# A hybrid convolution and retention step on one core: first weights in other pieces, taps scaled one sum later, the last head's norm ahead of its gate, and the feed-forwards' first job by k tiles

## The chip, the core and the metric

The kernel runs on one core of one Trainium2 chip. The core has a matrix engine (TensorE, PE in the profile; PEld is its weight load), VectorE (DVE), ScalarE (ACT), GpSimd (POOL) and SyncE (SP), which work side by side and meet through semaphores; each takes its own instructions in order. Matrix products end in PSUM, everything else lies in SBUF, and inputs come from memory by DMA, which SP, ScalarE or GpSimd start. The metric is the device time of one execution, in microseconds (us), lower is better.

## The reference

One inference step of a two-layer decoder over 544 tokens (512 of a prompt, 8 sequences of 4 sample tokens) with 1024 features, all in fp32:

```
x = x + short_conv_mixer(rmsnorm(x))      # layer 0: b, c, h = split(x @ w_in); u = c*h
                                          # y = sum_j w_conv[j] * u shifted by j; out = (b*y) @ w_out
x = x + swiglu(rmsnorm(x))                # (silu(x @ w_gate) * (x @ w_up)) @ w_down
x = x + retention_mixer(rmsnorm(x))       # layer 1: 4 heads, chunks of 128 tokens, a state S per head,
                                          # a norm over each head's output, a silu gate, @ w_out
x = x + swiglu(rmsnorm(x))
y = rmsnorm(x)
```

Returned are y for both groups of tokens, the last convolution inputs and the retention states.

## The kernel before

**Numbers.** An fp32 value is held as two reduced fp32 parts, a rounded high part (wh, oh, h: a copy by ScalarE, L202 or L326) and the low rest (wl, ol, l: a subtraction by VectorE, L203 or L327). A product of two values is three matmuls: high by high, high by low, low by high. Activations are stored feature by token; a matmul takes a 128x128 weight tile and half of the tokens, 272 (HT). `split` makes both parts; `mixed` makes the high part on ScalarE, then the low part half on VectorE and half through a DMA of GpSimd that adds the source to the negated high part (L328, L329).

**Jobs of seven products.** Most projections pair two 128-row blocks of weights and two blocks of operands and compute the 2x2 block product with seven products in place of eight (class `Job`, L375; products named 1 to 7, summed in L397). `weights7` (L331) makes the sums of weight blocks on VectorE (L347 to L350) and their parts. A job runs as `begin` (product 1), `middle` (5, 6, 2 in an order given to `run`, L433, for the first job, then 7) and `end` (3, 4); `take` names the results u1, u2, p5, c11, u3, c12 and c21, which ScalarE copies (L456) or VectorE adds to others (L458). Each product runs over four pairs of k tiles (KP = 4; KT = 8 k tiles of 128 features).

**Order.** The kernel is a straight program without loops on the chip. A scheduler orders each engine's queue from the order of the text, the tile pools' buffers and explicit constraints (`tc.issue_after(x.ins)`: behind instruction x). A constraint in one place can therefore also move instructions some distance away.

**Start and convolution (L464 to L681).** `start` (L481) loads x by eight k tiles (L502) and the first three weight blocks in pieces: k tile 0, tiles 1 to 3, tiles 4 to 7. All but one of the weight pieces go through SP's queue (L157), which lets eight loads be under way: a further one waits for the load eight places ahead. `split_x` scales and splits each k tile of x (L221, L222). The three projections then go k tile by k tile (L187). Two more `products` (L522) run on whole pieces, each piece split in one go (1024 wide). `square_sum` (L229) adds squares of x (L234 to L240) for the norm, `rms_scale` (L259) sums them over the features by matmuls (L275), takes the power on GpSimd (L250) and spreads it by matmuls (L256). The rest of the stage are jobs: for each pair of feature blocks one for c, one for h, and one for b. After an h job, VectorE forms u = c*h (L635, L636) and `taps` (L568) the convolution's sum y (L572, L574), which it then multiplies by the norm factor R (L583, L584); the b job's result is multiplied by y at its end (L589, L590).

**Feed-forwards (L684 on, one for each layer).** `operand` (L775) makes the parts for a k tile: scaling of x (L782), sums and differences of its blocks (L317 to L320), and their parts, 816 and 544 wide (L202, L203). A k tile of x is itself finished only by the stage ahead (L305 adds its projection). A loop (L884 to L890) calls `operand` and `square_sum` for each k tile in the order PAIRED[layer], whose last two are 6 and 7; the last square sum stands behind the last operand's parts. The first job's middle products run in the order 5, 2, 6 in the second layer and 5, 6, 2 in the first, each over all four k pairs.

**Retention (heads loop, L1603 to L1704).** For each head, chunks of 128 tokens are projected, multiplied, normalised (`normal`, L1419; its multiplication is L1422), gated (`gated`, L1447; L1460) and transposed; `states_update` (L1524) adds to the states (L1541). The function `inside` (L1684) is called from the next projection and holds the gating of chunk 2, the normal of chunk 3 and its state update, in this order. Normals use tiles of the tag yn, two buffers.

Of the kernel before, what the change touches and what calls it, by code (L numbers as in the profile page):

```python
# [12 lines left out]
P = 128  # L13
D = 1024
KT = D // P
SEQ = 512
# [36 lines left out]
def hybrid_decode_kernel(ctx: ExitStack, tc: tile.TileContext, a: dict, o: dict):  # L53
# [276 lines left out]

    def weights7(src1, src2, sw, n, adding=False, spare=None, first=1, fourth=False, whole=False):  # L331

# [13 lines left out]
        s2, s1 = w2[:, :n], w2[:, n:]  # L346
        nc.vector.tensor_add(s1, a21, a22)  # L347
        nc.vector.tensor_sub(s2, s1, a11)
        nc.vector.tensor_sub(a21, a11, a21)
        nc.vector.tensor_sub(w4, a12, s2)  # L350

# [7 lines left out]
        p3 = parts2(2 * n)  # L359
        mixed(*p3, w3, src2)  # L360
        p4 = parts2(n, sw, ("h4", "l4"))
# [13 lines left out]
    class Job:  # L375
# [14 lines left out]

        def product(self, out, which, first):
            wh, wl = self.w[which]
            for j, k in enumerate(self.ks):
                c = slice(j * P, (j + 1) * P)
                bh, bl = self.operand(k, which)
                for i, (w, b) in enumerate(((wh, bh), (wh, bl), (wl, bh))):
                    last = nc.tensor.matmul(  # L397
                        out, w[:, c], b,
                        start=(first and j == 0 and i == 0), stop=(j == len(self.ks) - 1 and i == 2),
                        skip_group_check=True,  # L400
                    )
                if which not in (5, 6, 2):
                    with tc.issue_after(last.ins):
                        next(self.weave, None)

        def begin(self):
            self.a = bank()[:, :HT]
            self.product(self.a, 1, True)
            self.take("u1", self.a)

        def middle(self):
            for which in self.order:
                if which == 6:
                    self.product(self.a, 6, False)
                    self.take("u2", self.a)
                elif which == 5:
                    self.c = self.third()[:, :HT]
                    self.product(self.c, 5, True)
                    self.take("p5", self.c)
                else:  # L420
                    self.b = bank()[:, :HT]
                    self.product(self.b, 2, True)
                    self.take("c11", self.b)
# [9 lines left out]
    def run(jobs, order, after, steps):  # L433
# [4 lines left out]
        for i, job in enumerate(jobs):  # L438
# [7 lines left out]
            after(i)  # L446

    def summed(dst, finish):


        def take(what, src):
# [5 lines left out]
            elif what in more:  # L457
                nc.vector.tensor_add(more[what], more[what], src)  # L458
            finish(what, src)
# [5 lines left out]
    with ExitStack() as c0:  # L465
# [15 lines left out]
        def start():  # L481


            pieces = [load_piece(a["cvin"][j], KT * P, parts=True) for j in range(3)]
            parts = [slice(0, P), slice(P, KP * P), slice(KP * P, KT * P)]
            nc.sync.dma_start(x[0], a["xT"][0])
# [13 lines left out]
            for kt in range(1, KT):  # L500
                steps.append(lambda kt=kt: split_x(kt, g_mix(0, kt)))
                nc.sync.dma_start(x[kt], a["xT"][kt])  # L502
                if kt in (1, 3):
                    for p in pieces:
                        p[2](parts[1 + kt // 3])
                        steps.append(lambda p=p, kt=kt: p[3](parts[1 + kt // 3]))
            last = steps[0]()
# [14 lines left out]
        def products(f, js, weave=iter(())):  # L522
            pts = []
            for j in js:
                wh, wl = load_piece(a["cvin"][3 * f + j], KT * P)
                pt = psum()
# [40 lines left out]

        def taps(f, scaled=True):  # L568

# [10 lines left out]
            )  # L580
            if scaled:
                r = R.rearrange("p a b -> p (a b)").unsqueeze(1).to_broadcast([P, 2, T])
                nc.vector.tensor_mul(y[:, :, NSLOT:], y[:, :, NSLOT:], r[:, :, :SEQ])  # L583
                nc.vector.tensor_mul(slots(y)[..., :DS], slots(y)[..., :DS], tokens(r))  # L584
            return y

        def mixed_in(b, y, f):
# [37 lines left out]
        def job(f, j):  # L625
            def take(what, src):
                if what != "c21":
                    return
# [29 lines left out]
        with ExitStack() as order:  # L658
            for last in (last_x[0], last_x[1], last_square[0]):
                order.enter_context(tc.issue_after(last.ins))  # L660
            for k in range(KP):
                operand_sums(k)
        mixed_in(b, taps(0, False), 0)
        run(jobs, (2, 5, 6), lambda i: None, iter(()))
# [19 lines left out]
    def ffn(layer, next_gain, then=None):  # L684
        with ExitStack() as c1:
# [198 lines left out]
            for kt in PAIRED[layer]:  # L884
                made = operand(kt)
                with ExitStack() as held:
                    if kt == KT - 1:
                        held.enter_context(tc.issue_after(made.ins))
                        held.enter_context(tc.issue_after(last_low[0].ins))
                    square_sum(kt, None, add=nc.vector)  # L890
            def after(i):
# [3 lines left out]
            steps = rms_scale(rest=9)  # L895
            run(jobs, (5, 2, 6) if layer else (5, 6, 2), after, steps)
            drain(steps)
# [223 lines left out]
    with ExitStack() as c2:  # L1121
# [296 lines left out]

        def normal(src, mv, rs):  # L1419

            yn = tp.tile([P, DV], F32, tag="yn", name=nm("yn"), bufs=2)
            last_normal[0] = nc.vector.tensor_scalar(yn, src, mv[:, 0:1], rs, op0=ALU.subtract, op1=ALU.mult)  # L1422
# [180 lines left out]
        for h in range(NH):  # L1603
# [79 lines left out]

            def inside():  # L1684
                with tc.issue_after(last_product[0].ins):
                    gated(h, st, yn2, 2)
                st["yn3"] = normal(p3, last, scale)
                states_update(h, st, 3, last_normal[0])
# [133 lines left out]
```

## Time and profile before

| what | value |
|---|---|
| median of 3 runs | 1389.73 us (1389.16 to 1390.19) |
| the profiled execution | 1392.42 us, span 1390.6 us |
| granted TensorE clock | 0.999 |
| busy: TensorE, VectorE, ScalarE, GpSimd | 1378.3, 1132.9, 823.4, 218.6 us |
| memory read and written | 191.31 and 28.42 MB |

The page counts an engine as busy while an instruction of its own is in it; TensorE's matmuls overlap, and a 128x128 by 272 matmul that waits for nothing starts every 0.125 us though its own time is about 0.29. A row of the timeline begins with its start and its duration in us, counted from the start of the span; then engine, line, operation, and output <- inputs with partitions x elements. In brackets stands how long the engine idled before it and what released it. "x3" is a run of three such instructions, and the duration is that of the run. A stall of TensorE of a microsecond is 0.07% of the time.

### The profile page before, as it was taken

The numbers are of one execution on the slowest core, as the hardware profiler recorded it, in microseconds if no ns is written. First come the engines' busy times: TensorE is split into PE (matmuls) and PEld (weight loads), VectorE is DVE, ScalarE is ACT, GpSimd is POOL, SyncE is SP. The second block draws the span as 40 slices with busy tenths as digits, with TensorE's granted clock in tenths as the row PEclk, the third lists the DMA queues.
The fourth block names the chain that finished last, engine by engine and source line by source line (L and its number), as shares of the span: only waits on it lengthen the run. The fifth ranks groups of instructions, "written<-read, shape, count | busy, mean of one in ns | idle before, by whom it ended". The sixth has DMA issues, their size and how long they took to land.

```text
span 1390.6 us, 26494 instructions
## 1 busy us (share of the span) xinstructions
PE 1378.3 (99%) x10427; PEld 1314.9 (95%) x10427; DVE 1132.9 (81%) x1925; ACT 823.4 (59%) x1284; POOL 218.6 (16%) x249
## 2 busy tenths in 40 slices
PE   9999999999999999999999999999999999999998
PEld 8999999999999999999978887887899999999997
DVE  6988789898989878777868586586799898989875
ACT  6666567767667656767641413224377767667654
POOL 0111012212221213211200000000112212221212
PEclk9999999999999999999999999999999999999999
DMA  6476346777777754777566455475766777777752
GB/s 208 113 179 154 121 108 154 171 174 171 152 183 166 165 126 122 195 180 221 175 237 230 148 187 202 134 258 183 220 137 153 171 172 174 154 180 167 164 111 88
DMA packets 99005, 233.15 MB, mean 168 GB/s; under 512 B 9760, under 2 KB 33456, under 8 KB 98496
## 3 DMA queue, kind: packets, MB, share of 16 engines
q1 hardware_dynamic: 68032, 167.47, 38.5%
q0 software_dynamic: 28400, 56.09, 23.5%
q10 hardware_dynamic: 2448, 7.91, 1.5%
q8 instruction: 81, 1.33, 0.4%
q14 instruction: 44, 0.36, 0.1%
HBM read 191.31 MB, written 28.42 MB: 158 GB/s over the span
## 4 chain that ended last, share of the span: by engine, by line
PE 94%; DVE 3%; DMA 1%; ACT 1%; issue 0%; POOL 0%; SPq 0%; DVEq 0%; ACTq 0%; POOLq 0%
PE sm L397 43%; PE mm L397 16%; PE mm L187 14%; PE sm L187 5%; PE sm L1267 2%; PE sm L1268 2%; PE sm L1269 2%; PE sm L175 2%; PE sm L176 1%; PE sm L177 1%; PE sm L1517 1%; PE mm L1278 1%; PE mm L1535 1%; PE mm L1445 1%; DMA w<-in_cvin_dram 0%
## 5 line engine op out<-in xcount | busy, mean ns | idle before, releaser
L397 PE MATMUL sm<-oh,wh 128*128 128x272 f32 x856 | 247.8, 290 | 2.0 <-ACT oh L202 1.5
L397 PE MATMUL sm<-ol,wh 128*128 128x272 f32 x856 | 246.2, 288 | 0.0
L397 PE MATMUL sm<-oh,wl 128*128 128x272 f32 x856 | 246.0, 287 | 0.0
L202 ACT ACTIVATE h<-w 128x1024 fp32r<-128x1024 f32 (+3 forms) x170 | 136.5, 803 | 91.1 <-PE mm L397 77.6
L203 DVE TENSOR_TENSOR l<-w,h 128x1024 fp32r<-128x1024 f32 (+3 forms) x170 | 153.6, 905 | 21.8 <-ACT h L202 19.7
L397 PEld LDWEIGHTS sm<-oh,wh 128*128 128x128 f32 x856 | 161.3, 188 | 3.5 <-ACT oh L202 1.8
L397 PEld LDWEIGHTS sm<-oh,wl 128*128 128x128 f32 x856 | 161.1, 188 | 0.0
L397 PEld LDWEIGHTS sm<-ol,wh 128*128 128x128 f32 x856 | 160.8, 188 | 0.2
L326 ACT ACTIVATE wh<-w 128x1024 fp32r<-128x1024 f32 (+1 forms) x132 | 131.8, 998 | 48.8 <-PE sm L397 40.8
L202 ACT ACTIVATE wh<-w 128x1024 fp32r<-128x1024 f32 (+3 forms) x78 | 70.0, 903 | 126.8 <-PE mm L187 61.2
L397 PE MATMUL sm<-parts,wh 128*128 128x272 f32 x736 | 142.6, 288 | 0.0
L329 POOL DMA_DIRECT2D wl<-in_ffgu_dram x87 | 81.9, 941 | 323.2 <-ACT wl L328 141.4
L397 PEld LDWEIGHTS sm<-parts,wh 128*128 128x128 f32 x736 | 115.5, 188 | 0.0
L397 PE MATMUL mm<-oh,h 128*128 128x272 f32 x396 | 114.0, 288 | 0.0
L397 PE MATMUL mm<-oh,l 128*128 128x272 f32 x396 | 113.4, 286 | 0.0
L397 PE MATMUL mm<-ol,h 128*128 128x272 f32 x396 | 113.1, 286 | 0.0
L397 PE MATMUL sm<-parts,wl 128*128 128x272 f32 x368 | 106.0, 288 | 0.0
L328 ACT ACTIVATE wl<-wh 128x512 fp32r<-128x512 f32 (+1 forms) x171 | 101.7, 595 | 2.2
L327 DVE TENSOR_TENSOR wl<-w,wh 128x512 fp32r<-128x512 f32 (+1 forms) x132 | 85.9, 651 | 17.8 <-ACT wh L326 17.5
L203 DVE TENSOR_TENSOR wl<-w,wh 128x1024 fp32r<-128x1024 f32 (+3 forms) x78 | 82.0, 1060 | 18.3 <-ACT wh L202 18.0
L187 PE MATMUL mm<-parts,wh 128*128 128x272 f32 x488 | 82.4, 291 | 1.7 <-ACT wh L202 1.3
L397 PE MATMUL sm<-oh,h 128*128 128x272 f32 x284 | 82.1, 289 | 0.0
(380 smaller groups left out, 3827.9 us busy)
## 6 DMA issues: line engine op xcount, KB each, us to landing
w<-in_ffgu_dram SPq DMA_DIRECT2D x66, 512.0 KB
wl<-in_ffgu_dram POOLq DMA_DIRECT2D x87, 256.0 KB, 5.4
S<-in_rets_dram SPq DMA_DIRECT2D x16, 1024.0 KB
out_rets_dram<-S SPq DMA_DIRECT2D x16, 1024.0 KB
w<-in_ffdn_dram SPq DMA_DIRECT2D x36, 384.0 KB
cb<-in_ffgu_dram SPq DMA_DIRECT2D x22, 512.0 KB
w<-in_cvin_dram SPq DMA_DIRECT2D x21, 512.0 KB
wl<-in_ffdn_dram POOLq DMA_DIRECT2D x48, 192.0 KB, 4.7
```

The costliest lines, as they stand in the source:

```text
L175: nc.tensor.matmul(out, lh, rh, start=start, stop=False, skip_group_check=True)
L187: last_product[0] = nc.tensor.matmul(half(pt, hf)[:, :HT], w[:, c], act[k][:, hf * HT : (hf + 1) * HT], start=(first and k == ks[0] and i ...
L202: h = nc.scalar.activation(dh, src, AF.Copy)
L203: last_low[0] = nc.vector.tensor_sub(dl, src, dh.bitcast(F32))
L326: nc.scalar.activation(wh, w, AF.Copy)
L327: last_mixed[0] = nc.vector.tensor_sub(wl[:, :n], w[:, :n], wh[:, :n].bitcast(F32))
L328: nc.scalar.activation(wl[:, n:], wh[:, n:].bitcast(F32), AF.Copy, scale=-1.0)
L329: nc.gpsimd.dma_start(wl[:, n:], src[:, 1, :] if len(src.shape) == 3 else src[:, n:], accum_op=ALU.add)
L397: last = nc.tensor.matmul(out, w[:, c], b, start=(first and j == 0 and i == 0), stop=(j == len(self.ks) - 1 and i == 2), skip_group_check= ...
L1267: nc.tensor.matmul(out, xh[kt][:, ts_], wh[:, cw], start=(kt == 0), stop=False)
L1268: nc.tensor.matmul(out, xh[kt][:, ts_], wl[:, cw], start=False, stop=False)
L1269: last = nc.tensor.matmul(out, xl[kt][:, ts_], wh[:, cw], start=False, stop=(kt == KT - 1))
```

## The change

Five things are done, all on the order of work or on the size of pieces.

- The first weights come in four pieces (k tile 0, tile 1, tiles 2 and 3, tiles 4 to 7) instead of three.
- In `products` the first piece of a call is split in two halves of 512, loaded as before in one.
- `taps` no longer multiplies by R; a new `scaled` does, called when the next b job's c11 has been added, behind that addition.
- A new `parted` runs the feed-forwards' first job: product 5, products 6 and 2 over the first three k pairs, then 6 and 2 over the last. The square sum of the last but one k tile moves behind the last tile's operand, and the second job's weight sums (`later`) and one of its splits stand behind that operand too.
- In the last head `inside` calls `normal` ahead of `gated`, with a tile of the tag rt1.

The diff, cut:

```diff
--- before.py
+++ after.py
-    def weights7(src1, src2, sw, n, adding=False, spare=None, first=1, fourth=False, whole=False):
+    def weights7(src1, src2, sw, n, adding=False, spare=None, first=1, fourth=False, whole=False, later=()):
...
-        nc.vector.tensor_add(s1, a21, a22)
-        nc.vector.tensor_sub(s2, s1, a11)
-        nc.vector.tensor_sub(a21, a11, a21)
-        nc.vector.tensor_sub(w4, a12, s2)
+        with ExitStack() as behind:
+            for made in later:
+                behind.enter_context(tc.issue_after(made.ins))
+            nc.vector.tensor_add(s1, a21, a22)
+            nc.vector.tensor_sub(s2, s1, a11)
+            nc.vector.tensor_sub(a21, a11, a21)
+            nc.vector.tensor_sub(w4, a12, s2)
...
-        mixed(*p3, w3, src2)
+        with ExitStack() as after:
+            for made in later:
+                after.enter_context(tc.issue_after(made.ins))
+            mixed(*p3, w3, src2)
...
-        def product(self, out, which, first):
+        def product(self, out, which, first, js=None):
             wh, wl = self.w[which]
-            for j, k in enumerate(self.ks):
+            for j in range(len(self.ks)) if js is None else js:
+                k = self.ks[j]
...
+        def parted(self):
+            n = len(self.ks) - 1
+            self.c = self.third()[:, :HT]
+            self.product(self.c, 5, True)
+            self.take("p5", self.c)
+            self.b = bank()
+            self.b = self.b[:, :HT]
+            self.product(self.a, 6, False, range(n))
+            with tc.issue_after(self.last.ins):
+                self.product(self.b, 2, True, range(n))
+            with tc.issue_after(self.last.ins):
+                self.product(self.a, 6, False, [n])
+            self.take("u2", self.a)
+            with tc.issue_after(self.last.ins):
+                self.product(self.b, 2, True, [n])
+            self.take("c11", self.b)
+
         def middle(self):
+            if not self.order:
+                self.parted()
             for which in self.order:
...
-                nc.vector.tensor_add(more[what], more[what], src)
+                last_add[0] = nc.vector.tensor_add(more[what], more[what], src)
...
-            parts = [slice(0, P), slice(P, KP * P), slice(KP * P, KT * P)]
+            cuts = (0, 1, 2, KP, KT)
+            parts = [slice(i * P, j * P) for i, j in zip(cuts, cuts[1:])]
...
-                if kt in (1, 3):
+                if kt in cuts:
+                    c = parts[cuts.index(kt)]
                     for p in pieces:
-                        p[2](parts[1 + kt // 3])
-                        steps.append(lambda p=p, kt=kt: p[3](parts[1 + kt // 3]))
+                        p[2](c)
+                        steps.append(lambda p=p, c=c: p[3](c))
...
-                wh, wl = load_piece(a["cvin"][3 * f + j], KT * P)
+                wh, wl, load, parted = load_piece(a["cvin"][3 * f + j], KT * P, parts=True)
+                load()
+                for c in ((slice(0, KP * P), slice(KP * P, KT * P)) if j == js[0] else (slice(0, KT * P),)):
+                    parted(c)
...
-        def taps(f, scaled=True):
+        def taps(f):
...
-            if scaled:
-                r = R.rearrange("p a b -> p (a b)").unsqueeze(1).to_broadcast([P, 2, T])
-                nc.vector.tensor_mul(y[:, :, NSLOT:], y[:, :, NSLOT:], r[:, :, :SEQ])
-                nc.vector.tensor_mul(slots(y)[..., :DS], slots(y)[..., :DS], tokens(r))
             return y
+
+        def scaled(y):
+            r = R.rearrange("p a b -> p (a b)").unsqueeze(1).to_broadcast([P, 2, T])
+            nc.vector.tensor_mul(y[:, :, NSLOT:], y[:, :, NSLOT:], r[:, :, :SEQ])
+            nc.vector.tensor_mul(slots(y)[..., :DS], slots(y)[..., :DS], tokens(r))
...
+                if j == 0 and what == "c11":
+                    with tc.issue_after(last_add[0].ins):
+                        scaled(pair["y"])
...
                     if kt == KT - 1:
+                        jobs[1].places["later"] = made, last_low[0]
                         held.enter_context(tc.issue_after(made.ins))
                         held.enter_context(tc.issue_after(last_low[0].ins))
-                    square_sum(kt, None, add=nc.vector)
+                    if kt == PAIRED[layer][-2]:
+                        continue
+                    for k in PAIRED[layer][-2:] if kt == PAIRED[layer][-1] else [kt]:
+                        square_sum(k, None, add=nc.vector)
...
-            run(jobs, (5, 2, 6) if layer else (5, 6, 2), after, steps)
+            run(jobs, (), after, steps)
...
-        def normal(src, mv, rs):
-
-            yn = tp.tile([P, DV], F32, tag="yn", name=nm("yn"), bufs=2)
+        def normal(src, mv, rs, tag="yn"):
+
+            yn = tp.tile([P, DV], F32, tag=tag, name=nm("yn"), bufs=2 if tag == "yn" else 1)
...
             def inside():
+                if not more:
+                    st["yn3"] = normal(p3, last, scale, "rt1")
                 with tc.issue_after(last_product[0].ins):
                     gated(h, st, yn2, 2)
-                st["yn3"] = normal(p3, last, scale)
+                if more:
+                    st["yn3"] = normal(p3, last, scale)
                 states_update(h, st, 3, last_normal[0])
```

More of the change, by code (lines that the diff above doesn't have):

```diff
@@ L401, in product @@
                     )
+                self.last = last
                 if which not in (5, 6, 2):
@@ L446, in run @@
             after(i)
+    last_add = [None]
     def summed(dst, finish):
@@ L662, in hybrid_decode_kernel @@
                 operand_sums(k)
-        mixed_in(b, taps(0, False), 0)
+        mixed_in(b, taps(0), 0)
         run(jobs, (2, 5, 6), lambda i: None, iter(()))
```

## The prediction

> **What bounds the kernel now.** I read the head of the page first, then the chain that ended last, then TensorE's waits, then the timeline around each wait.
>
> ```profile
> span 1390.6 us, 26494 instructions
> ...
> PE 1378.3 (99%) x10427; PEld 1314.9 (95%) x10427; DVE 1132.9 (81%) x1925; ACT 823.4 (59%) x1284; POOL 218.6 (16%) x249
> ...
> PE 94%; DVE 3%; DMA 1%; ACT 1%; issue 0%; POOL 0%; SPq 0%; DVEq 0%; ACTq 0%; POOLq 0%
> ```
>
> TensorE works 1378.3 of 1390.6 us and carries 94% of the chain. The change leaves its matmuls alone in number and shape (the same instructions in another order), so only the places where TensorE stands still can move. They are few:
>
> ```profile
> PE sm L397 <- ACT oh L202: 1.5, 1, 1.5
> PE mm L187 <- ACT wh L202: 1.3, 2, 1.1
> ...
> PE mm L397 <- ACT b L456: 0.6, 1, 0.6
> PE sm L397 <- DVE b L458: 0.5, 1, 0.5
> PE mm L187 <- DVE S L1541: 0.4, 1, 0.4
> ```
>
> The columns are the waiting instruction, what released it, total us, count, longest. These five lines sum to 4.3 us. Each part of the change aims at one of them, and each stall also costs the few matmuls behind it some 0.1 us, as the timeline shows below. So the question is which of them go, and what is late next. Nothing here can be worth more than about 7 us, 0.5%.
>
> **The first weights, now cut at k = 1, 2, 4.** The timeline of the start, one engine after the other:
>
> ```profile
> 7.45 0.41 PE L187 MATMUL sm<-parts,wl 128*128 128x272 f32 x2
> 8.99 0.93 PE L187 MATMUL mm<-parts,wh 128*128 128x272 f32 x4 [1.12 <-ACT wh L202]
> ...
> 4.69 0.29 ACT L202 ACTIVATE wh<-w 128x128 fp32r<-128x128 f32 x1
> ...
> 7.78 0.75 ACT L221 ACTIVATE parts<-x,vec 128x544 fp32r<-128x544 f32 x1 [1.98 <-DMA x<-in_xT_dram]
> 8.43 1.43 ACT L202 ACTIVATE wh<-w 128x384 fp32r<-128x384 f32 x3
> ...
> 8.29 0.33 SPq L502 DMA_DIRECT2D x<-in_xT_dram  x1
> ```
>
> What came last is the landing of x1: ScalarE idled 1.98 us for it, split x1 at 7.78, and then rounded the first 384-wide weight piece, some 0.50 us. With 128 columns that takes 0.29, so TensorE starts about 0.2 earlier, and one shorter VectorE split behind it adds 0.1: +0.3 us, while x1 lands as before. If x1 also lands earlier, since less weight data stands beside it, the whole wait of 1.1 and its 0.2 behind may go: +1.3. Against that stand three more loads on SP, 0.33 each: 1.0 us later for all behind. One k tile is 18 matmuls (three pieces, three products, two halves) at 0.125, 2.25 us, which covers it if k = 2's smaller pieces land in time; half of the 1.0 uncovered is the low end, -0.5. I take +0.3, nearest to the row for the 128-wide piece. The Trainium skill (DMA: Bandwidth & Descriptors, section Bandwidth) speaks against such cutting: it calls transfers under 64 KB dominated by descriptors and measures 138 GB/s for 64 KB against 341 for 1 MB. A piece 128 columns wide is 64 KB, one 256 wide 128 KB, and by that rule the two in place of one of 192 KB would end later. No trace here has these pieces yet; the first rival below gives the case a time from rows.
>
> **Products with the first piece's split in halves.**
>
> ```profile
> 25.22 0.66 PE L187 MATMUL sm<-parts,wh 128*128 128x272 f32 x4
> 26.06 0.52 PE L187 MATMUL sm<-parts,wl 128*128 128x272 f32 x2 [0.18 <-DVE wl L203]
> ...
> 24.79 1.23 DVE L203 TENSOR_TENSOR wl<-w,wh 128x1024 fp32r<-128x1024 f32 x1 [2.36 <-ACT wh L202]
> ...
> 11.35 0.64 ACT L202 ACTIVATE wh<-w 128x512 fp32r<-128x512 f32 x1
> ```
>
> Four matmuls from 25.22 end their issue at 25.72, and wl comes at 26.02: 0.34 of waiting and 0.1 behind it. A half takes ScalarE 0.64, and VectorE a bit more than half of 1.23, say 0.7, so the half of wl is there by about 25.5: the stall goes, +0.45. Three pieces are split so; each costs VectorE 2 x 0.7 - 1.23, some 0.15 more, and ScalarE about as much, and both idle around here. The matmuls of the norm's square sum now stand six matmuls earlier in TensorE's queue and may meet their last sum, which takes up to all of the gain. I take +0.35, 0 to +0.45.
>
> **Taps scaled one sum later.**
>
> ```profile
> 110.55 0.52 PE L397 MATMUL mm<-parts,h 128*128 128x272 f32 x2 [0.56 <-ACT b L456]
> ...
> 115.18 0.39 PE L397 MATMUL sm<-oh,wh 128*128 128x272 f32 x1 [0.46 <-DVE b L458]
> ...
> 107.75 1.40 ACT L572 ACTIVATE y<-u,vec 128x560 f32<-128x560 f32 x2
> ...
> 109.17 1.04 ACT L326 ACTIVATE wh<-w 128x1024 fp32r<-128x1024 f32 x1
> 110.12 0.38 ACT L456 ACTIVATE b<-mm 128x272 f32<-128x272 f32 x1
> ...
> 93.28 1.29 DVE L632 TENSOR_TENSOR c<-c,sqlast 128x1088 f32<-128x1088 f32 x1
> 94.49 0.68 DVE L327 TENSOR_TENSOR wl<-w,wh 128x512 fp32r<-128x512 f32 x1
> ...
> 102.07 0.69 DVE L348 TENSOR_TENSOR w<-w,w 128x512 f32<-128x512 f32 x1 [2.94 <-DMA w<-in_cvin_dram]
> ...
> 112.46 1.23 DVE L583 TENSOR_TENSOR y<-y,R 128x1024 f32<-128x1024 f32 x1
> ...
> 95.24 0.33 SPq L344 DMA_DIRECT2D w<-in_cvin_dram  x1
> ```
>
> Two stalls. At 110.55 the copy of p5 (L456) waited in ScalarE's queue behind the taps; in the new order the rounding of h and the taps trade places, less of the 1.40 and 1.04 above stands ahead, and I put the copy some 0.8 earlier: 0.56 and 0.1 go. At 115.18 the sum of u3 (L458) stands behind L583 (1.23) and two smaller instructions; only c11's sum has moved ahead of them, so u3's stays behind. But the order has moved further up too: L327 of 94.49, whose end lets SP issue the weight load of 95.24, now stands ahead of L632 (1.29). The load can go some 1.2 earlier, its data and the whole VectorE chain behind (it idled 2.94 for that load) with it. Then u3's sum is ready about when TensorE, itself earlier by what went upstream, arrives. Both stalls with their 0.1 each are 1.2 to 1.5. I take +1.1, since the second is a near tie; the high end is +1.5, the low end -0.7, one more 0.68 split ahead of that sum than now.
>
> **The feed-forwards' first job by k tiles.**
>
> ```profile
> 197.38 0.29 PE L397 MATMUL sm<-oh,wh 128*128 128x272 f32 x1
> 197.62 0.40 PE L397 MATMUL sm<-oh,h 128*128 128x272 f32 x1
> ...
> 1030.22 0.28 PE L397 MATMUL sm<-oh,wl 128*128 128x272 f32 x1
> 1032.04 0.39 PE L397 MATMUL sm<-oh,wh 128*128 128x272 f32 x1 [1.53 <-ACT oh L202]
> ...
> 1026.00 0.72 DVE L240 TENSOR_TENSOR sqacc<-sqacc,sqlast 128x544 f32<-128x544 f32 x1
> ...
> 1029.43 0.69 DVE L347 TENSOR_TENSOR w<-w 128x512 f32<-128x512 f32 x1
> ...
> 1032.29 1.64 DVE L203 TENSOR_TENSOR ol<-f,oh 128x816 fp32r<-128x816 f32 x2
> ...
> 1038.88 1.57 POOL L250 TENSOR_TENSOR rN<-rN,expo 128x5 f32<-128x5 f32 x1 [0.22 <-DVE rN L247]
> ...
> 1040.78 0.71 PE L256 MATMUL mm<-cb,rN 128*128 128x128 f32 x5
> ```
>
> In the first layer only slips like that of 197.62 remain (0.24 between starts where 0.125 is the rule), some 0.5 in all; the k order was nearly there before. I take +0.35, from -0.5 (the norm's sum one VectorE sum of 0.72 later) to +0.6.
>
> In the second layer TensorE issued 33 matmuls, then stood 1.7 us for the last k tile's operand, and some 0.2 more for the pieces behind. Parted, it has nine matmuls more to do first, 1.1 us. But it then asks at once for the operand's other part, which VectorE ends at 1033.93 (the second of the pair at 1032.29). With nothing else, that would end the job about 0.4 later than now. VectorE is the limit there, and three instructions leave its way: one L240 (0.72), L347 (0.69) and L348 (as L347), of which about 1.1 reaches the last operand, since x7's add and ScalarE's steps lie between. So -0.4 + 1.1 = about +0.6, from -0.4 to +1.9 (the whole stall). What is late next: the square sums stand behind the operand, and L247 behind a 1.22 split. Pool's power takes 1.57, so L247 may end until about 1039.2 before TensorE's L256 waits; I work it out at just that, hence no cost and a rival.
>
> **Last head's norm ahead of its gate.**
>
> ```profile
> 989.97 0.81 DVE L1422 TENSOR_SCALAR yn<-sm,mv,rs 128x512 f32<-128x512 f32 x1
> 990.69 2.34 DVE L1541 SCALAR_TENSOR_TENSOR S<-S,mm 128x1024 f32<-128x1024 f32 x2
> ...
> 991.96 0.77 PE L187 MATMUL mm<-parts,wh 128*128 128x272 f32 x4 [0.44 <-DVE S L1541]
> ```
>
> TensorE waits for the first of the two L1541. L1422 ahead of it moves into an earlier place, in a tile of its own, so L1541 ends 0.5 to 0.7 earlier and the wait of 0.44 with 0.1 behind it goes: +0.5. Its new place delays the state updates and sums ahead by 0.8, which had about that much room; if not, -0.3. High +0.65.
>
> **Sum.** 0.3 + 0.35 + 1.1 + 0.35 + 0.6 + 0.5 = 3.2 us; the low ends give -2.4, the high ends +6.4. The profiled execution took 1392.42 us, 1.8 us around its span and 2.7 above the median of 1389.73. So that execution would become 1389.2 and the median 1386.5.
>
> **Rivals.**
> First, the start gets slower. Its three added loads delay all behind by 1.0, and k = 2 waits: -0.9 instead of +0.3, 1387.7. For it: ScalarE's idle 1.98 shows that loads decide there. Against it: the 2.25 us a k tile. By the skill's rule on small transfers it is the likelier; I give 0.08.
> Second, the conv chain swallows what lies upstream. If the load of 95.24 does not move, u3's sum ends where it ends now, and all of start, products and taps (1.75) is waited for at 115. What remains is 1.45: 1388.3. For it: VectorE idles for that load. Against: L632's move. 0.18.
> Third, the stalls go wholly: the second layer's 1.9 instead of 0.6, and the start's 1.3 instead of 0.3, together 5.5: 1384.2. For it: TensorE has work without these operands. Against: VectorE's gapless queue and x1's landing. 0.20.
> Fourth, slower: the norm factor becomes the bound of both feed-forwards. If two long VectorE instructions (1.22 each) come ahead of L247 beyond what I counted, and nothing of the operand's 1.1 is seen, each layer loses 2.4 + 0.4 = 2.8; 2.25 - 5.6 = -3.4, so 1393.1. It decides from 1.1 of loss in each. For it: no room is left at L256. Against: L247's place in the queue shows only one such split. 0.12.
>
> **How the numbers follow.** My forecast holds 0.42, with 1385.3 to 1387.7 as its own range. 0.2% of the time, 2.8 us, is about what a measurement can tell from no change. The forecast's 0.42 falls 0.33 faster and 0.09 same; the third rival is faster; first and second are the same; the fourth is slower by over 0.2% in 0.09 and the same in 0.03. That is 0.53 faster, 0.38 same, 0.09 slower. The range, 1384.0 to 1389.7, leaves out the fourth rival and the outer part of the third.
>
> **What the profile would show.** TensorE's wait on wh drops to about 0.9 in total; those on b (ScalarE's copy and VectorE's sum) and on S leave the list or fall below 0.2; that on oh falls to about 1. The matmuls' busy time stays. A wait of L256 on rN, one of L275 on sqacc, one at k = 2 or 3 of the start, or a conv load issued no earlier than before relative to its stage would make me wrong.

## The result, and the profile after

The changed kernel took 1396.68 us in the median of 6 runs (1395.95 to 1397.50), the kernel before 1390.39 beside it (1389.16 to 1391.67): a ratio of 1.0045, with an interval of 1.0033 to 1.0058. I had forecast 1386.5, and the range ended at 1389.7. So a gain of 3.2 us was expected and a loss of 6.3 came.

The head of the page of the changed kernel:

```profile
span 1394.2 us, 26518 instructions
...
PE 1380.1 (99%) x10427; PEld 1316.3 (94%) x10427; DVE 1133.7 (81%) x1931; ACT 823.4 (59%) x1290; POOL 218.2 (16%) x249
```

TensorE has the same number of matmuls, but they were busy 1380.1 us rather than 1378.3. Where it stood still is in TensorE's waits of the changed kernel (who waited, for whom, us in total, times, longest):

```profile
PE sm L404 <- DMA wl<-in_cvin_dram: 3.4, 1, 3.4
PE mm L256 <- POOL rN L250: 1.7, 2, 1.1
...
PE sm L187 <- DVE yn L1464: 0.5, 1, 0.5
PE mm L187 <- ACT f L820: 0.4, 1, 0.4
PE sm L404 <- ACT g L485: 0.2, 1, 0.2
...
PE sm L404 <- DVE ol L203: 0.2, 1, 0.2
```

(L397 is now L404, L456 and L458 are L485 and L487.) All five waits of the kernel before that the prediction dealt with have left the list or fallen to 0.2. In their place stand two that are larger: 3.4 us for the DMA half of a weight's low part in the conv stage, and 1.7 us for the norm factor rN. The timeline of the changed kernel around the first, one engine after the other:

```profile
71.70 0.28 PE L404 MATMUL sm<-oh,wl 128*128 128x272 f32 x1
...
75.47 0.41 PE L404 MATMUL sm<-parts,wh 128*128 128x272 f32 x2
79.29 0.45 PE L404 MATMUL sm<-parts,wl 128*128 128x272 f32 x1 [3.40 <-DMA wl<-in_cvin_dram]
79.53 0.43 PE L404 MATMUL mm<-oh,l 128*128 128x272 f32 x1
79.76 0.43 PE L404 MATMUL mm<-oh,h 128*128 128x272 f32 x1
...
82.71 0.38 PE L404 MATMUL sm<-oh,wl 128*128 128x272 f32 x1
82.92 0.29 PE L404 MATMUL sm<-oh,wh 128*128 128x272 f32 x1
83.05 0.29 PE L404 MATMUL sm<-ol,wh 128*128 128x272 f32 x1
...
71.90 1.06 ACT L326 ACTIVATE wh<-w 128x1024 fp32r<-128x1024 f32 x1 [3.84 <-PE sm L404]
...
73.14 0.62 ACT L328 ACTIVATE wl<-wh 128x512 fp32r<-128x512 f32 x1
...
74.05 0.86 POOL L329 DMA_DIRECT2D wl<-in_cvin_dram  x1 [5.54 <-ACT wl L328]
```

The same steps in the kernel before, for the same weight (the first one of the third conv job):

```profile
72.17 0.29 PE L397 MATMUL sm<-oh,wl 128*128 128x272 f32 x1
...
84.30 0.41 PE L397 MATMUL sm<-parts,wh 128*128 128x272 f32 x2
84.54 0.29 PE L397 MATMUL sm<-parts,wl 128*128 128x272 f32 x1
...
72.37 1.06 ACT L326 ACTIVATE wh<-w 128x1024 fp32r<-128x1024 f32 x1 [0.88 <-PE sm L397]
...
74.53 0.87 POOL L329 DMA_DIRECT2D wl<-in_cvin_dram  x1 [3.56 <-ACT b L456]
```

In both kernels ScalarE waits for TensorE before it rounds this weight, because the buffer that the part goes into still holds an earlier part, last used by the matmuls up to 72.17 and 71.70. The steps behind are as long in both: rounding at 72.37 and 71.90, GpSimd's adding DMA 2.2 us later, at 74.53 and 74.05. So the part is made no later than before. It is asked for earlier: TensorE comes to its low part at 84.54 in the kernel before, some 12 us after the buffer's last use. In the changed kernel that matmul is due at 75.72, 4.0 us after it, and the DMA lands only at 79.29, 5.2 us after its issue. And once TensorE goes on, its matmuls start 0.227 us apart (79.53, 79.76) until 82.71, where 0.125 was the rule and is again. The windows of the changed kernel (span, busy us and count of PE, PEld, DVE, ACT, POOL; then granted clock, DMA share, GB/s) name the reason:

```profile
60.00:79.00 19.00, 15.88 (x124) 15.49 (x123) 15.91 (x26) 12.91 (x23) 3.48 (x4) 1.00 0.66 154
79.00:90.00 11.00, 10.71 (x73) 10.71 (x74) 6.71 (x11) 3.63 (x7) 0.33 (x1) 0.84 0.31 73
```

The granted clock fell to 0.84 in the mean over the 11 us behind the wait. Some 15 matmuls at 0.1 extra are 1.5 us. The next start was due at 75.72, two matmuls behind 75.47, and came at 79.29: 3.57. Together that is 5.1 us at one place.

### The profile page after: what moved, and what is told of

Read it like the earlier page. It is cut to its first block, busy times and chain, and to the rows that moved or that the text cites. A ratio compares the mean times of both kernels' runs of the same rounds, so it can differ in the third digit from the quotient of the medians.

```text
span 1394.2 us, 26518 instructions
## 1 busy us (share of the span) xinstructions
PE 1380.1 (99%) x10427; PEld 1316.3 (94%) x10427; DVE 1133.7 (81%) x1931; ACT 823.4 (59%) x1290; POOL 218.2 (16%) x249
## 5 line engine op out<-in xcount | busy, mean ns | idle before, releaser
L404 PE MATMUL sm<-oh,wh 128*128 128x272 f32 x856 | 247.4, 289 | 0.0
L404 PE MATMUL sm<-ol,wh 128*128 128x272 f32 x856 | 246.5, 288 | 0.0
L404 PE MATMUL sm<-oh,wl 128*128 128x272 f32 x856 | 246.1, 288 | 0.0
L203 DVE TENSOR_TENSOR l<-w,h 128x1024 fp32r<-128x1024 f32 (+3 forms) x170 | 153.4, 903 | 21.3 <-ACT h L202 19.3
L326 ACT ACTIVATE wh<-w 128x1024 fp32r<-128x1024 f32 (+1 forms) x132 | 131.8, 998 | 56.7 <-PE sm L404 46.4
L404 PEld LDWEIGHTS sm<-oh,wh 128*128 128x128 f32 x856 | 161.5, 189 | 1.3 <-DVE b L487 0.4
L404 PEld LDWEIGHTS sm<-oh,wl 128*128 128x128 f32 x856 | 161.2, 188 | 0.0
L404 PEld LDWEIGHTS sm<-ol,wh 128*128 128x128 f32 x856 | 161.0, 188 | 0.1
L404 PE MATMUL sm<-parts,wh 128*128 128x272 f32 x736 | 143.1, 288 | 0.0
L404 PEld LDWEIGHTS sm<-parts,wh 128*128 128x128 f32 x736 | 115.8, 189 | 0.0
L404 PE MATMUL mm<-oh,h 128*128 128x272 f32 x396 | 114.5, 289 | 0.0
L404 PE MATMUL mm<-oh,l 128*128 128x272 f32 x396 | 114.1, 288 | 0.0
L404 PE MATMUL mm<-ol,h 128*128 128x272 f32 x396 | 113.6, 287 | 0.0
L404 PE MATMUL sm<-parts,wl 128*128 128x272 f32 x368 | 106.5, 290 | 3.4 <-DMA wl<-in_cvin_dram 3.4
L328 ACT ACTIVATE wl<-wh 128x512 fp32r<-128x512 f32 (+1 forms) x171 | 101.8, 595 | 2.2
L327 DVE TENSOR_TENSOR wl<-w,wh 128x512 fp32r<-128x512 f32 (+1 forms) x132 | 85.6, 649 | 20.6 <-ACT wh L326 20.5
L203 DVE TENSOR_TENSOR wl<-w,wh 128x1024 fp32r<-128x1024 f32 (+3 forms) x84 | 82.6, 994 | 16.9 <-ACT wh L202 16.5
L404 PE MATMUL sm<-ol,h 128*128 128x272 f32 x284 | 82.0, 289 | 0.2 <-DVE ol L203 0.2
```

What stands on the lines that cost most here:

```text
L203: last_low[0] = nc.vector.tensor_sub(dl, src, dh.bitcast(F32))
L326: nc.scalar.activation(wh, w, AF.Copy)
L327: last_mixed[0] = nc.vector.tensor_sub(wl[:, :n], w[:, :n], wh[:, :n].bitcast(F32))
L328: nc.scalar.activation(wl[:, n:], wh[:, n:].bitcast(F32), AF.Copy, scale=-1.0)
L404: last = nc.tensor.matmul(out, w[:, c], b, start=(first and j == 0 and i == 0), stop=(j == len(self.ks) - 1 and i == 2), skip_group_check= ...
```

## The experiments

Each kernel ran between runs of the kernel before on the same chip, in three groups. The kernel before had a median of 1390.84 us beside the halves undone, the halves alone, the start alone and the feed-forward part undone. It had 1390.16 beside the other cut, the run of start, taps and head, the head alone and the feed-forward part alone, and 1389.57 beside the other three. The ratio given with each run is the one to compare by.

**The halved splits undone, alone, and with another cut.** Which part brought the wait is told apart by taking the halves out of the changed kernel and putting them alone into the kernel before.

```diff
 # changed kernel, halves undone
-                for c in ((slice(0, KP * P), slice(KP * P, KT * P)) if j == js[0] else (slice(0, KT * P),)):
+                for c in (slice(0, KT * P),):
                     parted(c)
```

> The changed kernel with only the halved splits in products undone. Theory: the halves alone reorder TensorE's queue in the first conv jobs, so that between the last use of one buffer of weight parts and the need of the parts that follow in it only 32 matmuls (4.0 us) remain instead of 97 (12.1 us); refilling takes about 8 us. Undone, TensorE's 3.4 us wait for wl (DMA) at 79 us and the lowered granted clock behind it (0.84 from 79 to 90 us) go: 5.1 us less, 0.4 given back at 24 us, so about 1392.0. Rival: the three added loads of the start or the later taps delay the DMA queue, and the wait stays with or without halves: 1396.7 or a little above.

Measured: 1390.93 us, a ratio of 1.0000 (0.9992 to 1.0009). Its windows:

```profile
79.00:90.00 11.00, 11.00 (x90) 11.00 (x89) 10.96 (x19) 7.50 (x13) 2.36 (x3) 1.00 0.57 134
```

90 matmuls in this stretch instead of 73, clock 1.00, and no wait for a DMA's wl in the whole run. The theory holds; the rival's 1396.7 is excluded.

The halves alone in the kernel before:

```diff
-                wh, wl = load_piece(a["cvin"][3 * f + j], KT * P)
+                wh, wl, load, parted = load_piece(a["cvin"][3 * f + j], KT * P, parts=True)
+                load()
+                for c in ((slice(0, KP * P), slice(KP * P, KT * P)) if j == js[0] else (slice(0, KT * P),)):
+                    parted(c)
```

> The kernel before with only the halved splits in products added. Theory: TensorE waits about 3.2 us for wl near 80 us (35 matmuls of room); 0.3 us are won at 26 us; if the clock falls behind a wait of that length, 1.5 more: 1393.2 to 1394.8. Rival (the wait comes from start or taps): no such wait, 1390.0.

Measured: 1395.33 us, a ratio of 1.0036 (1.0024 to 1.0049). Its timeline and window:

```profile
79.97 0.39 PE L404 MATMUL sm<-parts,wl 128*128 128x272 f32 x1 [2.96 <-DMA wl<-in_cvin_dram]
80.19 0.28 PE L404 MATMUL mm<-oh,l 128*128 128x272 f32 x1
80.32 0.29 PE L404 MATMUL mm<-oh,h 128*128 128x272 f32 x1
```

```profile
79.00:90.00 11.00, 10.03 (x80) 10.04 (x81) 8.32 (x15) 4.80 (x10) 1.48 (x2) 1.00 0.30 75
```

The wait is here with neither start, taps, head nor feed-forward changed: 2.96 us where 3.2 was expected. The clock behind it stayed at 1.00 in this traced run, and the matmuls are 0.13 apart from the second on. The time lies 0.5 above what I had expected at most. The mean granted clock of the traced run was 0.999, that of the four others 0.997 or 0.998, as in the six runs of the changed kernel (0.996 to 0.998); so the clock may have fallen in those, and 3.1 of waiting and 1.5 behind it would make 4.6, beside the measured 4.5. But 15 of the 83 runs of the kernel before beside these experiments also show 0.997 or 0.998, and only the traced run can be looked into, so this is a reading and not shown.

What of the halves does it, the added instructions or the order that follows from them? A cut of 768 and 256 columns, in the first call of products alone, adds one such split. In the order of TensorE's queue, the room between the last use of the old part and the need of the new one is then 97 matmuls as in the kernel before (12.1 us), and 32 (4.0 us) with 512 and 512. Refilling takes L326 1.06, L328 0.6 and the DMA 5.2 from its issue to the landing: with small waits between them, some 7.4 us from 71.90 to 79.29. That is 3.4 more than the room of 4.0, and 3.4 is the wait.

```diff
 # changed kernel with the feed-forward part undone, and in products:
-                for c in ((slice(0, KP * P), slice(KP * P, KT * P)) if j == js[0] else (slice(0, KT * P),)):
+                for c in ((slice(0, 6 * P), slice(6 * P, KT * P)) if j == js[0] and len(js) > 1 else (slice(0, KT * P),)):
```

> Start, taps and last head as changed; feed-forwards as before; and in the first call of products alone the first piece is split 768 and 256 wide instead of 512 and 512. By its queue order this other cut leaves TensorE's first conv jobs as they were (97 matmuls of room before the buffer of weight parts is needed again). Theory (the order is the cause, not the added split): no wait for wl near 80 us, granted clock 1.00 there; the stalls at 24 to 26 us of the run with the halves undone (1.2 us) fall below 0.5: about 1388.0. Rival (the added split itself delays ScalarE and VectorE, and with them the weights): the wait of 3.4 us and 1394 again.

Measured: 1389.73 us, 1.0001 (0.9992 to 1.0009); no wait for a DMA's wl, and in its window:

```profile
79.00:90.00 11.00, 11.00 (x89) 10.91 (x89) 10.76 (x20) 8.17 (x14) 1.59 (x3) 1.00 0.35 81
```

From 61 to 84 us TensorE's matmuls stand in the order of the kernel before. So one split in two does not cost this by itself, and with the old order the wait is gone. With the halves, and else the same kernel, the order was another, the wait 3.4 and the ratio 1.0024 (the feed-forward part undone, below). The halves split one piece in each of the three calls of products, though, and this run only one. That the other two splits make the part late is not what the timelines above show: its steps take as long in both kernels. The time was 1.7 above what I expected: the waits at 24 to 26 us are 0.30 and 0.22, together a little over the 0.5 I had set.

The chain itself: in the kernel with the halves alone, the part that came late is made wholly on VectorE, without the DMA.

```diff
 # kernel before with the halves, conv jobs:
-                spare=(None, lambda: sum_place)[turn[0] % 2],
+                spare=(None, lambda: sum_place)[turn[0] % 2], whole=turn[0] == 3,
```

> The kernel before with the halved splits, and with the first weights of the third conv job split wholly on VectorE, so that the part TensorE waited for at 80 us needs no DMA of GpSimd (some 5 us of the chain of 8 from the free buffer to the landed part). TensorE's order up to that job is that of the run with the halves alone. Theory (the chain buffer, rounding, negation, DMA sets the wait): the wait near 80 us falls below 0.7, granted clock 1.00: 1391.0 to 1392.0. Rival (something else in the reordered jobs is late, for instance the weight load itself): a wait of 2 us or more stays there: 1393.5 or more.

Measured: 1392.00 us, 1.0017 (1.0008 to 1.0026). The wait near 80 us is gone and the clock is 1.00:

```profile
79.00:90.00 11.00, 11.00 (x89) 10.87 (x88) 10.86 (x18) 6.77 (x14) 0.86 (x1) 1.00 0.36 85
```

That is what the theory said, but it does not prove it. In the traces TensorE's order is that of the run with the halves alone only up to 75.6 us here, 13 matmuls ahead of the place where that run waits. So the wait may be gone because of the order and not because the DMA is, and this run does not tell the two apart. The 2.4 us above the kernel before are not explained by stalls that its trace shows. A fourth buffer for the parts, meant to leave the order and take away the wait for the buffer, was not tried.

**The start alone.**

```diff
-            parts = [slice(0, P), slice(P, KP * P), slice(KP * P, KT * P)]
+            cuts = (0, 1, 2, KP, KT)
+            parts = [slice(i * P, j * P) for i, j in zip(cuts, cuts[1:])]
...
-                if kt in (1, 3):
+                if kt in cuts:
```

> The kernel before with only the first weights cut in four pieces. If the start's gain in the changed kernel's trace (1.7 us by 25 us, against the traced run of the kernel before) is real, about 1388.8. Rival: the kernel before had its x1 late only in the traced run, and its other runs have little to gain there: 1390.0 to 1390.4, with the traced stall at 9 us smaller than 1.1 in both.

Measured: 1389.91 us, 0.9998 (0.9989 to 1.0007): no change. The theory falls, and the rival only half holds. In the traces, the stall at 9 us depends on the run. TensorE's wait for wh there was 1.12 in the kernel before, and in other kernels with the same start 0.78, 0.73, 0.56, 0.42 and twice none. In the six with the new cuts none is listed at that place. But there is a new wait at 24 to 26 us, where the whole 1024-wide split of products comes last. The timeline of the kernel with the start alone:

```profile
24.09 0.77 PE L187 MATMUL sm<-parts,wh 128*128 128x272 f32 x4 [0.23 <-ACT wh L202]
25.36 0.52 PE L187 MATMUL sm<-parts,wl 128*128 128x272 f32 x2 [0.49 <-DVE wl L203]
```

0.7 us of waiting, against 0.18 listed before. In the changed kernel, with the halves, these two waits are gone, so the halves did here what was meant; the reordering took it away later.

**The taps alone.**

```diff
+                if j == 0 and what == "c11":
+                    with tc.issue_after(last_add[0].ins):
+                        scaled(pair["y"])
```

> The kernel before with only the taps scaled one sum later. TensorE's and ScalarE's queues are the same as before, and five places on VectorE differ. Theory: u3's sum still stands behind the multiplication, so the stalls at 110 and 115 us stay at 0.4 to 0.7 and 0.6: 1390.2, no change. Rival (as predicted, both stalls go): 1389.1.

Measured: 1389.78 us, 1.0001 (0.9993 to 1.0010). Both waits stay, the second smaller than the 0.56 of the kernel before:

```profile
PE sm L404 <- DVE b L487: 0.5, 1, 0.5
...
PE mm L404 <- ACT b L485: 0.2, 1, 0.2
```

The sum of u3 stands behind the multiplication as before, and no gain is measured. Nor is the smaller wait its doing: in the traces of the head alone and the feed-forward part alone, which leave the taps as they were, that wait is 0.3 and 0.2. In the changed kernel both waits were gone although the part does not remove them. That TensorE came some five microseconds late there could be a reason, but not the only one: the run of start, taps and head together (below) has no such delay, and its trace lists neither wait. The run with the halves undone, whose order on ScalarE and VectorE is the same up to there, lists 0.6 and 0.5. So these two stalls also differ from trace to trace.

**The last head alone, and start, taps and head together.**

```diff
             def inside():
+                if not more:
+                    st["yn3"] = normal(p3, last, scale, "rt1")
```

> The kernel before with only the last head's normal moved. In the traces the second feed-forward's wait of 1.7 us on its last operand is nearly gone (0.2) where this part stands without the feed-forward part, with a wait of 0.5 on rN in its place, and the stall of 0.6 at the head's end becomes one of 0.4 some earlier: about 1389.5. Rival (the feed-forward's wait depends on when the stage ahead ends and not on this part): 1390.3 to 1391, with a wait of 0.7 to 1.7 on oh in the second feed-forward.

Measured: 1390.95 us, 1.0004 (0.9995 to 1.0013). Its waits include:

```profile
PE sm L187 <- DVE yn L1456: 0.6, 1, 0.6
...
PE mm L256 <- POOL rN L250: 0.3, 1, 0.3
...
PE sm L404 <- DVE ol L203: 0.2, 1, 0.2
```

The wait for S (0.4) is replaced by one for yn, 0.6: a matmul that needs the PSUM tile which this instruction reads now waits for VectorE a little earlier than the other did. In the second feed-forward the wait on the last operand is small here (0.2, the last row), so my reading of the traces was right as far as it went, and a wait of 0.3 on rN took its place. In the time, none of it shows: it is the rival's.

```diff
 # changed kernel: products and feed-forwards as before
-                for c in ((slice(0, KP * P), slice(KP * P, KT * P)) if j == js[0] else (slice(0, KT * P),)):
+                for c in (slice(0, KT * P),):
...
-            run(jobs, (), after, steps)
+            run(jobs, (5, 2, 6) if layer else (5, 6, 2), after, steps)
...
```

> Start, taps and last head as changed; products and feed-forwards as before. It is the run above without the split. Theory: 1388.8, with stalls of 0.6 each at 24.5 and 25.8 us. Rival (the start's gain is not real): 1389.5 to 1390.5.

Measured: 1390.45 us, 1.0003 (0.9994 to 1.0011): the rival's end of the two. Of the two stalls expected, one is listed, 0.49 at 25.37. Three parts that each move a stall of about half a microsecond add up to nothing that can be measured.

**The feed-forward part undone, alone, and without its later weight sums.**

```diff
 # changed kernel, feed-forward part undone
-            run(jobs, (), after, steps)
+            run(jobs, (5, 2, 6) if layer else (5, 6, 2), after, steps)
...
-                        jobs[1].places["later"] = made, last_low[0]
...
```

> The changed kernel with the feed-forward part undone (first job in the old orders, square sums and next weight sums as before). By the traces the part loses 0.35 us in the first layer and 0.3 us in the second (the waits of L256 on rN, 0.8 and 1.2, outweigh the late operand): about 1396.0. Rival: the part is a gain as predicted (1.0): 1397.6. Second rival: part of what the runs lost beyond the traces (6.3 against 3.6 us) lies here: below 1394.5.

Measured: 1394.13 us, 1.0024 (1.0013 to 1.0035): 3.3 above the kernel before beside it, where the changed kernel was 6.3 above. That is on the second rival's side. The wait for wl (3.4) and the clock (0.84 from 79 to 90 us) are unchanged in it.

```diff
 # kernel before with the feed-forward part
+                        jobs[1].places["later"] = made, last_low[0]
...
-            run(jobs, (5, 2, 6) if layer else (5, 6, 2), after, steps)
+            run(jobs, (), after, steps)
...
```

> The kernel before with only the feed-forward part. Theory: the late rN costs 0.8 in the first layer and about 1.2 in the second, and what the last operand wins there is 1 to 1.7; the first layer loses 0.5, the second is even: 1391.3. Rival (the loss seen is that of the part together with the head's): 1389.9 as predicted, with L256 waiting below 0.3 in the second layer.

Measured: 1391.06 us, 1.0007 (0.9998 to 1.0016): by the interval from 0.3 us faster to 2.2 slower, and not the gain of 0.95 predicted. In its trace L256 waits for rN in the first layer (0.62) and not in the second, so the rival's condition is met there and its time is not. The wait of 1.5 on the second layer's last operand is gone. In its place, earlier in the first job, stands one that neither the theory nor the rival had:

```profile
1029.39 0.39 PE L404 MATMUL sm<-oh,h 128*128 128x272 f32 x1 [1.09 <-ACT g L485]
...
1028.44 0.61 ACT L328 ACTIVATE wl<-wh 128x512 fp32r<-128x512 f32 x1
1028.96 0.38 ACT L485 ACTIVATE g<-sm 128x272 f32<-128x272 f32 x1
```

TensorE waits for ScalarE to copy a result out of PSUM (L485), and that copy stands in ScalarE's queue behind the negation of a weight's high part (L328).

```diff
 # kernel before with the feed-forward part, without
-                        jobs[1].places["later"] = made, last_low[0]
```

> The kernel before with the feed-forward part, but with the next job's weight sums left where they were. Theory (those sums, moved behind the last operand, stand ahead of L247 on VectorE and make rN late): the waits of L256 on rN, 0.8 in the first layer and about 0.6 in the second, fall to 0.2 or below, and the sums stand ahead of the last operand again, so that the second layer's wait on it is 0.7 or more: 1390.5. Rival (the later square sum makes rN late): L256 waits as long as with the whole part, 1391.1.

Measured: 1390.79 us, 1.0008 (0.9999 to 1.0017), which does not tell the two apart by time. The traces do, in the first layer. The kernel with the whole part, GpSimd and TensorE:

```profile
204.08 0.86 POOL L329 DMA_DIRECT2D wl<-in_ffgu_dram  x1 [7.86 <-ACT wl L328]
204.64 2.01 POOL L250 TENSOR_TENSOR rN<-rN,expo 128x5 f32<-128x5 f32 x1
...
206.70 0.76 PE L256 MATMUL mm<-cb,rN 128*128 128x128 f32 x5 [0.62 <-POOL rN L250]
```

Without the later weight sums:

```profile
201.58 0.86 POOL L329 DMA_DIRECT2D wl<-in_ffgu_dram  x1 [5.43 <-ACT u L485]
203.96 1.20 POOL L250 TENSOR_TENSOR rN<-rN,expo 128x5 f32<-128x5 f32 x1 [1.51 <-DVE rN L247]
```

In the first, the power L250 stands in GpSimd's queue behind the issue of the adding DMA, which had waited for ScalarE's negation until 204.08, since the split that it belongs to was held behind the last operand; in the second that issue is 2.5 us earlier and the wait in the first layer is gone. In the second layer the theory fails: without the later weight sums L256 waits 0.4 there, where the whole part had no such wait, and the wait on the last operand that I expected (0.7 or more) is not listed.

## Why the prediction was wrong, step by step

**Products with halves: the step that failed.** I had it at +0.35, from 0 to +0.45. It is a loss: 1.0036 alone, that is 5.0 us on 1390 (3.3 to 6.8 by the interval, and 4.5 between the medians). At 24 to 26 us it does what I said. What I left out is that the halves changed the order of TensorE's queue in the conv jobs 40 us later, and with it the room between the last use of a buffer of weight parts and the need of the part that refills it: 4.0 us in place of 12.1, where refilling takes 7.4. I knew that the orders there were reshuffled, and in the taps step I counted only the half of it that helps (the weight load of 95.24 earlier). I did not follow the ring of three buffers for the weight parts: who uses the part last, and how long refilling takes. The refill can be had from the rows of the kernel before: L326 1.06, then the negation, then the DMA of about 5 us. Against it stand the 32 matmuls of 0.125 of the new order.

**The clock, not in the prediction at all.** I priced a stall at its length and 0.1 behind it. A wait of 3.40 us was followed by 3.4 us of matmuls 0.227 apart, 1.5 us more, and one of 3.37 in the run with the feed-forward part undone in the same way; one of 2.96 us was not. The Trainium skill (TensorE: Matmul & The Clock Gate, section What's actually happening) says that the clock gate goes to half after an idle window of about 3.4 us, and its section Back-to-back issue gap gives N/1.2 ns for the gated state, by which 272 columns are estimated at 0.227 us. The spacing seen, 0.227, agrees. As to the window, 3.40 and 3.37 lie at it and 2.96 below; these three traces fit the page, but do not settle where the limit is.

**The start (+0.3).** 0.9998 alone, from 1.5 us faster to 1.0 slower. The size fits a bound, but not the reasoning: I took the stall of one traced run for the kernel's own. Other traces of the same start show 0 to 0.8, and the split of products is the next limit. My first rival (the loads end later) did not come: with the smaller pieces no wait stands at 9 us. The Trainium skill's rule that transfers under 64 KB are dominated by their descriptors (DMA: Bandwidth & Descriptors, section Bandwidth) ends just below the new pieces of 64 and 128 KB (pieces of 64 KB were in the kernel before too, as its k tile 0), and these traces show no cost of them.

**Taps (+1.1).** No gain: 1.0001 alone, from 1.0 us faster to 1.4 slower. I had seen that u3's sum stays behind the multiplication, and then let the earlier load repair it. The load's place follows from the order that the other parts make, not from this one: with the taps alone L327 still stands behind the 1.28 us multiplication (L632 in the kernel before), as before.

**Feed-forwards (+0.35 and +0.6).** A loss of about 1.0 alone, or none by its interval (0.9998 to 1.0016). The fourth rival named a mechanism that came, rN late, at 2.4 us a layer and a chance of 0.12; in the changed kernel it measured 0.61 in the first layer and 1.06 in the second. With the part alone the second is missing, and the wait of 1.09 for ScalarE's copy stands there; with the head alone rN is 0.33 late. So the 1.06 is not this part's alone. The step that failed is "I work it out at just that, hence no cost": in the changed kernel L247 stood behind that split, three more instructions and a wait. The timeline of the changed kernel in the second layer:

```profile
1038.86 1.17 PE L275 MATMUL mm<-cb,sqacc 128*128 128x1 f32 x10
...
1039.76 1.22 DVE L203 TENSOR_TENSOR l<-w,h 128x1024 fp32r<-128x1024 f32 x1
1040.90 0.68 DVE L327 TENSOR_TENSOR wl<-w,wh 128x512 fp32r<-128x512 f32 x1
1041.50 0.43 DVE L487 TENSOR_TENSOR g<-g,sm 128x272 f32<-128x272 f32 x1
1043.22 0.69 DVE L203 TENSOR_TENSOR l<-w,h 128x512 fp32r<-128x512 f32 x1 [1.29 <-ACT h L202]
1043.83 0.16 DVE L247 TENSOR_SCALAR rN<-mm 128x5 f32<-128x5 f32 x1
```

The sum that L247 reads ended at 1040.03 (L275). The last L203 ahead of it waited 1.29 us for ScalarE, and L247 waited with it until 1043.83. In the first layer it was GpSimd's queue, which I had not looked at for this step.

**Last head (+0.5).** 1.0004 alone, from 0.7 us faster to 1.8 slower: the wait moved from S to yn.

**What stays open.** The two traced runs are 3.5 us apart, the medians 6.3: the traced run of the kernel before was the slowest of its runs (1392.42, with a stall of 1.1 us at 9 us that is smaller or absent in others), that of the changed kernel its fastest (1395.95). Of the 6.3, 5.1 are the wait and the clock; undoing the halves brought back 6.2 against the kernel before beside it. About 1 us is not placed, nor are the 2.4 us of the run with the part made on VectorE. The parts do not add up either: undoing the feed-forward part brought back 3.0 with the halves, and without them nothing (1.0000 with it and 1.0003 without). Why is open. Single runs of one kernel spread over 1.5 to 4 us, so single traces cannot settle that. Of the versions tried none is measurably faster than the kernel before; the lowest ratio is 0.9998, of the start alone.

## What to carry to other kernels

When a change lets a scheduler reorder a later stage, follow each ring of buffers there: from the last use in the new order, add the steps that refill it, and compare with the matmuls until the new part is needed. In an in-order queue, an instruction that waits holds up all that stand behind it, so look for the small urgent instruction (here the norm factor) behind a large one that waits. And take no stall of half a microsecond from one trace as the kernel's own: what depends on when a DMA lands must be seen in several runs.

## What the runs showed of the hardware

In a kernel that is 99% busy, the granted clock fell after a wait of 3.40 us (0.84 from 79 to 90 us), in another kernel after one of 3.37, and in a third not after one of 2.96. It stayed low for about as long as the wait was (matmuls 0.227 apart from 79.3 to 82.7 us, 0.125 from 82.9). An adding DMA of GpSimd for 128x512 fp32 took 5.2 us from its issue to the matmul that waited for it (74.05 to 79.29).
